# Where the residual of a feed-forward is fetched and added: a change in the order of loads around seven block products

## The chip, the core and the metric

The kernel runs on one core of a Trainium2 chip, as one launch. The metric is the device time of that core in microseconds, as the median of several runs. A core has TensorE for matrix products (PE; its weight loads are listed as PEld), VectorE (DVE), ScalarE (ACT), GpSimd (POOL) and SyncE (SP), which here issues nearly all DMAs. Every engine works through its own instructions in order and waits on semaphores.

## What is computed

One layer of a decoder trunk on 1024 prompt tokens and 64 sample tokens: a half-step feed-forward, a token mixer, a second half-step feed-forward and a last norm.

```python
def swiglu(x, w_in, w_out):
    gu = x @ w_in
    g, u = gu[..., :D_FF], gu[..., D_FF:]
    return (jax.nn.silu(g) * u) @ w_out
...
x = x + 0.5 * swiglu(rmsnorm(x, norm_ffn1[l]), ffn1_w_in[l], ffn1_w_out[l])
...
x = x + mix
x = x + 0.5 * swiglu(rmsnorm(x, norm_ffn2[l]), ffn2_w_in[l], ffn2_w_out[l])
```

D_MODEL is 1024 and D_FF is 2816. All inputs are float32. The change is in code that both feed-forwards use, so it acts twice.

## The kernel before

**Tokens and precision.** The 1088 tokens are two halves of 512 and 576, and each half is once more two equal parts of columns (256 or 288). Activations lie transposed: 128 channels on the partitions, tokens along the free axis. A float32 product is made from three float32r products: each operand is split into a high part (ScalarE's copy into float32r) and a low part (VectorE's subtraction of the high part from the source), and high x high, high x low and low x high are summed in PSUM.

**First product of a feed-forward (`ffn_in`, L546, and `wino`, L476).** Each hidden tile of 128 channels is made by Winograd's variant of Strassen's method: seven block products instead of eight, in the order 1, 2, 6, 5, 7, 3, 4 (L42). They share three PSUM banks, A for 1, 6, 7 and 4, B for 2, and C for 5 and 3. So a bank's sum must be copied out before a later product may add to it. The function `after0` (L550) does so for the first half: behind product 2 VectorE adds (L565), GpSimd adds the two column parts (L562), and ScalarE makes the SiLU (L567); behind product 6 ScalarE copies bank A into v (L569). Product 7, two products after 6, adds to A again. Most hidden tiles are made for both halves in one go, so that `xs` has two entries. The last tile (number 21) is made for one half after the other, each with a single entry in `xs`. This is the "one-half tile". `after0` has the first half alone, so its one-half tile comes once in each feed-forward.

**Second product (`second`, L740).** The product with `w_out` uses the same method, over pairs of hidden tiles, in the order 1, 2, 5, 6, 4, 7, 3 (L744). For each of the first six there are four units m = 0 to 3, written (p,m) below. Such a unit is 11 steps k of three matmuls for each of the two halves, 66 matmuls. Its weights come in three blocks kb = 0, 4 and 8; the generator `weights` (L791) loads raw tiles (`raw`, L770, issue L774), sums them on GpSimd where the method asks for it (L805, L809, L814; after product 4 also `fourth`, L821), and splits the sum (`parts`, high part on ACT L787, low part on DVE L788). The operands X of a product are 11 tiles each, hidden sums that the kernel had written to DRAM: `fetch_X` (L750) loads them (L760, named hr or hp) and `split_X` (L764) splits them on ACT (L767) and DVE (L768). For the next product, up to three tiles are fetched after each unit (L921 and L922), and the rest before that product begins (L905).

**Leaving a unit (`leave`, L858).** Each unit's two PSUM results are scaled by 0.5 and added on VectorE (L863) to four accumulators. These are a and b for the output tiles m and 4 + m, each with two token parts f and s.

**Residual parts.** The residual x lies in DRAM (`xspill`). One quarter of it, for b in part s, is loaded straight into the accumulator after product 6 (L882). The other three quarters go through a tile xo: `old` (L823) loads it with two DMAs (L827), and a GpSimd add (L833) follows later. `old` is called after a unit of product 6 (a, part f), and twice after a unit of product 7 (b part f, a part s). The list `late_` keeps the adds until the next unit has gone through its last weight block, kb = 8 (L852).

**What sets the order of instructions.** The kernel is written as one Python program. The framework's planner then gives each engine its order: at each point it takes, of the instructions whose inputs and buffers are ready by its own reckoning, the one traced first. So instructions with free inputs and buffers, weight loads above all, move ahead of what stands before them in the text. `pin` (`keep_in_program_order`) holds one instruction behind the instruction that was traced last on the same engine. The GpSimd adds and sums of the second product are all pinned, and so are the xo loads and ACT's high parts of X; L882 is not. Buffers come in rings by tag: `act` has 42 buffers (for hr and hh of most steps, xo, the weight sums that several products need, and more), `pair` has 8 (hp), `wraw` 6 (raw weights), `wsum` 4. `tick` (L159) only starts side work, such as norms and output transposes, when the kernel's own count of TensorE time has reached it.

**The end of the second product.** After product 7, `run` (L899) adds what is left in `late_`, calls `half` for each half (it starts the next norm, or in the second feed-forward the output transposes, named ptf), and does product 3 for one half after the other.

Of the kernel before, what the change touches and what calls it, by code (L numbers as in the profile page):

```python
# [11 lines left out]
AF = mybir.ActivationFunctionType  # L12
# [53 lines left out]
def tile_hybrid_pool_ssd_macaron(  # L66
# [11 lines left out]
    dma = nc.sync.dma_start  # L78
# [467 lines left out]
    def ffn_in(wi, ff, xs):  # L546

        out = {}

        def after0(p, i, bk):  # L550

            A, B, C = bk
            n = NPAIR[0]
            f, s_ = slice(0, n), slice(n, 2 * n)
            if p == "1":
                out[i] = o = {"g": fx(name="g"), "t": fx(name="t"), "v": fx(name="v")}
                S.copy(o["t"][:, : 2 * n], A)
                return
            g, t, v = out[i]["g"], out[i]["t"], out[i]["v"]

            def halves(o, x):
                G.tensor_tensor(o, x[:, f], x[:, s_], op=ALU.add)  # L562

            if p == "2":
                V.tensor_tensor(g[:, : 2 * n], B, t[:, : 2 * n], op=ALU.add)  # L565
                halves(g[:, f], g)
                S.activation(g[:, f], g[:, f], AF.Silu)  # L567
            elif p == "6":
                S.copy(v[:, : 2 * n], A)  # L569
            elif p == "5":  # L570
                S.copy(t[:, : 2 * n], C)
            elif p == "7":
                V.tensor_tensor(t[:, : 2 * n], A, t[:, : 2 * n], op=ALU.add)
                halves(t[:, f], t)
            elif p == "3":
                V.tensor_tensor(v[:, : 2 * n], C, v[:, : 2 * n], op=ALU.add)
                halves(g[:, s_], v)
                S.activation(g[:, s_], g[:, s_], AF.Silu)
            else:
                S.copy(t[:, s_], A[:, s_])  # L580
                V.tensor_tensor(t[:, s_], A[:, f], t[:, s_], op=ALU.add)
                V.tensor_tensor(g[:, f], g[:, f], t[:, s_], op=ALU.mult)
                G.tensor_tensor(g[:, s_], g[:, s_], t[:, f], op=ALU.mult)
                hidden(0, ff, g)

        def after(p, i, bk):
            h = xs[i][0]
            if h == 0:
                return after0(p, i, bk)
            n = NPAIR[h]  # L590
            A, B, C = (b[:, :n] if b is not None else None for b in bk)
            if p == "1":
                t = fx(name="t")
                out[i] = o = {"g": fx(name="g"), "t1": t[:, :n], "t5": t[:, :n], "t2": t[:, n : 2 * n]}
                S.copy(o["t1"], A)
                return
            o = out[i]
            g1, g2 = o["g"][:, :n], o["g"][:, n : 2 * n]
            if p == "2":
                V.tensor_tensor(g1, B, o["t1"], op=ALU.add)  # L600
                S.activation(g1, g1, AF.Silu)
            elif p == "6":
                S.copy(o["t2"], A)
            elif p == "5":
                S.copy(o["t5"], C)
            elif p == "7":
                V.tensor_tensor(o["t5"], A, o["t5"], op=ALU.add)
            elif p == "3":
                V.tensor_tensor(g2, C, o["t2"], op=ALU.add)
                S.activation(g2, g2, AF.Silu)  # L610
            else:
                V.tensor_tensor(g1, g1, A, op=ALU.mult)
                G.tensor_tensor(g2, g2, o["t5"], op=ALU.mult)
                hidden(h, ff, o["g"])

        wino(wino_weights(wi, 0, 4, 4, ff * P, FF + ff * P), 4, xs, after)
# [123 lines left out]
    def second(wo, after, half):  # L740
# [4 lines left out]
        X = {p: [] for p in order}  # L745
        T1 = [None] * 4
        xt = [[None] * KD for _ in HALVES]
        raws, held, late_ = [], {}, []

        def fetch_X(p, n):  # L750
            for k in range(len(X[p]), min(len(X[p]) + n, NK2)):
# [69 lines left out]
                pin(G.tensor_tensor(a, x, a, op=ALU.subtract))  # L821

        def old(m, q, col):  # L823
            t = act((P, 576), name="xo")
            for h in HALVES:
                n, at = NPAIR[h], HALF_AT[h]
                pin(dma(t[:, at : at + n], xspill[h][4 * q + m][:, col * n : (col + 1) * n]))  # L827

            def put():
                for h in HALVES:  # L830
                    n, at = NPAIR[h], HALF_AT[h]
                    o = xt[h][4 * q + m][:, col * n : (col + 1) * n]
                    pin(G.tensor_tensor(o, o, t[:, at : at + n], op=ALU.add))  # L833

            late_.append(put)

        def unit(p, m, hs, ws):
            pts = [psum("pd", "po" + p)[:, : NPAIR[h]] for h in hs]
            for kb, nk, wh, wl in ws:
                if kb and len(hs) == 2 and (p, m) == ("1", 0):  # L840
                    split_X(kb + 4)
                elif kb == 8:
                    split_X()
                for kk in range(nk):
                    k = kb + kk
                    for j, (W_, lo_) in enumerate(((wh, 0), (wh, 1), (wl, 0))):
                        for h, pt in zip(hs, pts):
                            at = HALF_AT[h]
                            mm(pt, W_[:, kk, :], X[p][k][lo_][:, at : at + NPAIR[h]],
                               start=k == 0 and j == 0, stop=k == NK2 - 1 and j == 2)  # L850
                    tick()
                if kb == 8:  # L852
                    while late_:
                        late_.pop(0)()
            for h, pt in zip(hs, pts):
                leave(p, m, h, pt)

        def leave(p, m, h, pt):  # L858
            n, at = NPAIR[h], HALF_AT[h]
            f, s_ = slice(0, n), slice(n, 2 * n)  # L860

            def add(out, prior):
                V.scalar_tensor_tensor(out, pt, 0.5, prior, op0=ALU.mult, op1=ALU.add)  # L863

            if p == "1":
                if T1[m] is None:
                    T1[m] = act((P, 576), name="t1")
                S.activation(T1[m][:, at : at + n], pt, AF.Copy, scale=0.5)
                return
            if p == "2":  # L870
                xt[h][m] = fx(name="x")
            elif p == "5":
                xt[h][4 + m] = fx(name="x")
            t, a, b = T1[m][:, at : at + n], xt[h][m], xt[h][4 + m]
            if p == "2":
                add(a[:, f], t)
            elif p == "5":
                add(b[:, s_], t)
            elif p == "6":
                add(a[:, s_], b[:, s_])  # L880
                add(b[:, f], t)
                dma(b[:, s_], xspill[h][4 + m][:, s_])  # L882
            elif p == "4":
                add(b[:, f], b[:, f])
                pin(G.tensor_tensor(b[:, s_], b[:, s_], a[:, s_], op=ALU.add))
            elif p == "7":
                add(b[:, f], b[:, f])
                add(b[:, s_], b[:, s_])
            else:
                add(a[:, s_], a[:, s_])  # L890
# [8 lines left out]
        def run(side):  # L899
            fetch_X("1", NK2)  # L900
            split_X(4)
            for p, nxt in zip(order[:-1], order[1:]):
                if p != "1":
                    split_X(8)
                fetch_X(p, NK2)  # L905
                for m in range(4):
                    unit(p, m, HALVES, weights(p, m))
                    if p == "6":
                        old(m, 0, 0)
                    elif p == "7":  # L910
                        old(m, 1, 0)
                        old(m, 0, 1)
                    if p == "4":
                        fourth(m)
                    if side and p == "2" and m == 0:
                        finish(side)
                    while p == "1" and hlast:
                        hlast.pop(0)()
                    while p == "1" and m == 2 and hsums:
                        finish(hsums.pop(0))  # L920
                    n = AHEAD[nxt] - len(X[nxt])  # L921
                    fetch_X(nxt, min(n, 3))  # L922
            split_X(8)
            fetch_X("3", NK2)
            while late_:
                late_.pop(0)()
            for h in HALVES:
                half(h, xt[h])
            kept = {m: [] for m in range(4)}

            def keep(m):
                for w in weights("3", m):
                    kept[m].append(w)
                    yield w

            for h in HALVES:
                for m in range(4):
                    unit("3", m, [h], kept[m] if h else keep(m))
                after(h, xt[h])
# [1080 lines left out]
```

## Time and profile before

| | |
|---|---|
| median of 3 runs | 2925.12 us (2923.38 to 2926.3) |
| the profiled execution's own time | 2925.94 us |
| its span, first to last instruction | 2924.2 us |
| mean granted TensorE clock in it | 0.985 |
| second product of the first feed-forward | from 527 us, with its last unit's results leaving at 800 us |
| second product of the second feed-forward | from 2639 us, with its last unit's results leaving at 2909 us |

A row of a timeline reads: start, duration, engine, line of the kernel, operation, output<-inputs, shape, how many were merged, and in brackets how long the engine had been idle and what ended that. An engine name with q, such as SPq, means an instruction of its queue: SP's DMA issues are there, and their duration is that of the issue, not of the transfer. A row of windows gives for one stretch of the span each engine's busy time and number of instructions, then the granted TensorE clock (1.00 is full speed), the mean busy share of the 16 DMA engines and what they moved. A row for one line of the kernel gives the shortest, median and longest duration in ns.

### The profile page before, as it was taken

How to read it: one execution, taken by the hardware profiler on the slowest of the kernel's cores; microseconds unless marked ns; L12 is line 12 of the kernel's file. 1: busy time of each engine (PE TensorE's matmuls, PEld its weight loads, DVE VectorE, ACT ScalarE, POOL GpSimd, SP SyncE). 2: the span in 40 equal slices, each digit the busy share in tenths (PEclk: the TensorE clock that was granted, in tenths of full speed). 3: DMA queues.
4: the chain of work that ended last, by engine and by line, in shares of the span. 5: the costliest groups of instructions: out<-in, count | busy, mean ns of one | idle time of the engine just before them, and what ended most of it. 6: DMA issues, size and time to landing. Idle time of an engine off the chain costs nothing. (4 is left out here: it accounts for less than half of the span.)

```text
span 2924.2 us, 54556 instructions
## 1 busy us (share of the span) xinstructions
PE 2798.1 (96%) x19834; PEld 2614.3 (89%) x19834; DVE 1857.1 (64%) x2848; ACT 1400.7 (48%) x3086; POOL 1370.1 (47%) x1424
## 2 busy tenths in 40 slices
PE   7999999998999999999999999898999999999987
PEld 6999999998889999999998887677999999999987
DVE  6656556666884586866766767766665444456675
ACT  5444444433444555554555566566233344444333
POOL 6456566146542364554622333332235676561562
PEclk9999999999999999999999999999999999999999
DMA  4466445677545455543366577785774333246783
GB/s 132 147 196 210 158 147 177 209 216 234 167 115 170 150 179 169 184 140 125 101 234 214 186 230 240 248 263 185 241 238 136 114 118 102 88 132 192 214 241 105
DMA packets 567437, 515.25 MB, mean 176 GB/s; under 512 B 37876, under 2 KB 436072, under 8 KB 567160
## 3 DMA queue, kind: packets, MB, share of 16 engines
q1 hardware_dynamic: 564848, 507.31, 55.3%
q10 hardware_dynamic: 2320, 4.46, 0.4%
q8 instruction: 156, 2.56, 0.4%
q14 instruction: 113, 0.93, 0.1%
HBM read 363.51 MB, written 148.36 MB: 175 GB/s over the span
## 5 line engine op out<-in xcount | busy, mean ns | idle before, releaser
L167 PE MATMUL pw<-X,wh 128*128 128x288 f32 (+2 forms) x2832 | 626.2, 310 | 4.0 <-ACT v L569 4.0
L167 PEld LDWEIGHTS pw<-X,wh 128*128 128x128 f32 x2832 | 462.0, 189 | 26.2 <-ACT v L569 4.8
L167 PE MATMUL pw<-X,wl 128*128 128x288 f32 (+1 forms) x1644 | 473.3, 288 | 0.0
L167 PE MATMUL pw<-hl,wh 128*128 128x256 f32 (+1 forms) x1536 | 395.2, 330 | 0.6 <-ACT wh L452 0.4
L453 DVE TENSOR_TENSOR wl<-s,wh 128x512 fp32r<-128x512 f32 x288 | 232.0, 807 | 253.7 <-ACT wh L452 241.7
L446 POOL TENSOR_TENSOR s<-wraw,wraw 128x512 f32<-128x512 f32 x144 | 199.5, 1386 | 337.7 <-DVE wl L453 224.0
L167 PE MATMUL pw<-hi,wh 128*128 128x288 f32 x1120 | 331.2, 296 | 0.0
L167 PE MATMUL pw<-hi,wl 128*128 128x288 f32 x1120 | 330.4, 295 | 0.0
L167 PE MATMUL pw<-lo,wh 128*128 128x288 f32 x1120 | 330.2, 295 | 0.0
L167 PEld LDWEIGHTS pw<-X,wl 128*128 128x128 f32 x1644 | 311.7, 190 | 0.0
L167 PE MATMUL pw<-hl,wl 128*128 128x256 f32 x1072 | 301.8, 282 | 1.2 <-DVE wl L453 1.2
L167 PEld LDWEIGHTS pw<-hl,wh 128*128 128x128 f32 x1536 | 260.4, 190 | 22.0 <-ACT wh L452 0.6
L452 ACT ACTIVATE wh<-s 128x512 fp32r<-128x512 f32 x288 | 181.1, 630 | 163.9 <-PE pw L167 139.9
L453 DVE TENSOR_TENSOR wl<-wraw,wh 128x512 fp32r<-128x512 f32 x216 | 170.5, 789 | 135.8 <-ACT wh L452 127.2
L452 ACT ACTIVATE wh<-wraw 128x512 fp32r<-128x512 f32 x216 | 135.6, 628 | 174.6 <-PE pw L167 151.4
L167 PEld LDWEIGHTS pw<-hi,wh 128*128 128x128 f32 x1120 | 211.2, 189 | 6.4
L167 PEld LDWEIGHTS pw<-lo,wh 128*128 128x128 f32 x1120 | 211.2, 189 | 0.0
L167 PEld LDWEIGHTS pw<-hi,wl 128*128 128x128 f32 x1120 | 210.7, 188 | 0.0
L167 PEld LDWEIGHTS pw<-hl,wl 128*128 128x128 f32 x1072 | 204.7, 191 | 1.4 <-DVE wl L453 1.4
L167 PE MATMUL po<-hr,wh 128*128 128x256 f32 (+1 forms) x848 | 188.2, 293 | 10.3 <-DVE hr L768 10.2
L167 PE MATMUL po<-hh,wh 128*128 128x256 f32 (+1 forms) x848 | 186.8, 291 | 6.7 <-ACT hh L767 6.3
L167 PE MATMUL po<-hh,wl 128*128 128x256 f32 (+1 forms) x848 | 186.0, 290 | 0.5 <-DVE wl L788 0.3
(400 smaller groups left out, 6850.8 us busy)
## 6 DMA issues: line engine op xcount, KB each, us to landing
wraw<-in_ffn_w_in_dram SPq DMA_DIRECT2D x188, 256.0 KB
wraw<-in_w_in_dram SPq DMA_DIRECT2D x144, 256.0 KB
wh<-part SPq DMA_DIRECT2D x116, 256.0 KB
wl<-part SPq DMA_DIRECT2D x116, 256.0 KB
hr<-hb SPq DMA_DIRECT2D x106, 272.0 KB
wraw<-in_ffn_w_out_dram SPq DMA_DIRECT2D x96, 256.0 KB
hb<-g SPq DMA_DIRECT2D x66, 288.0 KB
hb<-g SPq DMA_DIRECT2D x66, 256.0 KB
```

What stands on the lines that cost most here:

```text
L167: T.matmul(out, lhsT, rhs, start=start, stop=stop, skip_group_check=free)
L446: G.tensor_tensor(t, a, b, op=op)
L452: S.activation(wh, a, AF.Copy)
L453: V.tensor_tensor(wl, a, wh.bitcast(F32), op=ALU.subtract)
```

## The change

Three edits, all in code that both feed-forwards run.

1. In `after0`, when the tile is made for one half alone, the SiLU of part f is no longer issued behind product 2, but behind product 6, pinned after the copy of bank A.
2. `old` no longer loads. It puts a function (`reload_`, the former body) on a list `olds`. The load of the quarter that goes straight into b (L882) goes on that list as well, and is now pinned. The list is worked off in the next unit, behind the matmuls of its block kb = 4; working it off also puts the adds on `late_`.
3. `late_` is worked off behind the last weight block of a unit, after the loop. After product 7, both lists are emptied before `half`.

```diff
             if p == "2":
                 V.tensor_tensor(g[:, : 2 * n], B, t[:, : 2 * n], op=ALU.add)
                 halves(g[:, f], g)
-                S.activation(g[:, f], g[:, f], AF.Silu)
+                if len(xs) > 1:
+                    S.activation(g[:, f], g[:, f], AF.Silu)
             elif p == "6":
                 S.copy(v[:, : 2 * n], A)
+                if len(xs) == 1:
+                    tc.keep_in_program_order(S.activation(g[:, f], g[:, f], AF.Silu))
...
         def old(m, q, col):
+            olds.append(lambda: reload_(m, q, col))
+
+        def reload_(m, q, col):
             t = act((P, 576), name="xo")
             for h in HALVES:
                 n, at = NPAIR[h], HALF_AT[h]
...
                     tick()
-                if kb == 8:
-                    while late_:
-                        late_.pop(0)()
+                if kb == 4:
+                    while olds:
+                        olds.pop(0)()
+            while late_:
+                late_.pop(0)()
             for h, pt in zip(hs, pts):
                 leave(p, m, h, pt)
...
             elif p == "6":
                 add(a[:, s_], b[:, s_])
                 add(b[:, f], t)
-                dma(b[:, s_], xspill[h][4 + m][:, s_])
+                olds.append(lambda: pin(dma(b[:, s_], xspill[h][4 + m][:, s_])))
...
             fetch_X("3", NK2)
-            while late_:
-                late_.pop(0)()
+            for q in (olds, late_):
+                while q:
+                    q.pop(0)()
             for h in HALVES:
                 half(h, xt[h])
```

More of the change, by code (lines that the diff above doesn't have):

```diff
@@ L747, in second @@
         xt = [[None] * KD for _ in HALVES]
-        raws, held, late_ = [], {}, []
+        raws, held, late_, olds = [], {}, [], []
         def fetch_X(p, n):
```

## The prediction

> **What bounds the kernel now.** I read the page first, then TensorE's waits, then windows over the two places that the diff touches, then the timelines of SP, GpSimd (POOL), VectorE (DVE) and ScalarE (ACT) there.
>
> ```profile
> PE 2798.1 (96%) x19834; PEld 2614.3 (89%) x19834; DVE 1857.1 (64%) x2848; ACT 1400.7 (48%) x3086; POOL 1370.1 (47%) x1424
> PE po L167 <- ACT wh L787: 15.5, 7, 3.8
> PE po L167 <- DVE hr L768: 10.2, 20, 1.9
> PE po L167 <- ACT hh L767: 6.3, 5, 2.9
> PE pw L167 <- ACT v L569: 4.0, 3, 2.0
> ```
>
> TensorE is busy 96% of the span, so a change can only take away its waits and the stretches in which it runs slowly. The wait rows read: who waited, for whom, total us, times, longest. The matmuls of the second product carry the name po; their three largest waits sum to 32.0 us. The wait for the copy v (L569) is the half tile's.
>
> ```profile
> 576.00:592.00 16.00, 16.00 (x131) 16.00 (x130) 9.15 (x17) 6.87 (x12) 0.00 (x0) 1.00 0.55 160
> 644.20:757.10 112.90, 98.92 (x729) 96.45 (x728) 77.95 (x99) 38.43 (x67) 69.75 (x58) 0.94 0.75 219
> 2752.60:2865.30 112.70, 100.13 (x728) 97.05 (x727) 78.55 (x99) 37.79 (x66) 69.59 (x58) 0.94 0.74 220
> 677.70:691.80 14.10, 8.82 (x62) 7.95 (x61) 8.80 (x11) 2.97 (x6) 9.18 (x9) 0.96 0.69 209
> 691.80:716.60 24.80, 24.80 (x192) 24.75 (x191) 22.50 (x23) 9.89 (x17) 22.28 (x16) 0.96 0.75 214
> 716.60:737.40 20.80, 17.07 (x133) 16.42 (x131) 12.81 (x17) 6.45 (x12) 11.67 (x11) 1.00 1.04 300
> ```
>
> Columns: window, length, busy time (count) of PE, PEld, DVE, ACT, POOL, then granted clock, DMA share, GB/s. In products 2 and 5 TensorE takes 16.00/131 = 0.122 us per matmul, so a unit of 66 matmuls lasts 8.06 us. Products 6, 4 and 7, from the end of unit (6,0) to the end of (7,3), have 729 matmuls, worth 89.0 us, and take 112.9: 23.9 us too many in the first feed-forward, and 112.7 - 728 x 0.122 = 23.9 in the second. These 48 us are nearly all that the edit of the second product can win. I write (p,m) for unit m of product p.
>
> **The change part by part.** *The half tile's SiLU.*
>
> ```profile
> 508.06 0.42 ACT L567 ACTIVATE g<-g 128x256 f32<-128x256 f32 x1 [2.82 <-POOL g L562]
> 508.38 0.61 ACT L452 ACTIVATE wh<-s 128x512 fp32r<-128x512 f32 x1
> 508.90 0.56 ACT L569 COPY v<-pw 128x512 f32<-128x512 f32 x1
> 509.08 0.72 DVE L453 TENSOR_TENSOR wl<-s,wh 128x512 fp32r<-128x512 f32 x1 [1.64 <-ACT wh L452]
> 509.51 0.67 PE L167 MATMUL pw<-X,wh 128*128 128x512 f32 x1 [2.00 <-ACT v L569]
> 509.50:514.00 4.50, 4.49 (x17) 3.85 (x18) 3.33 (x4) 1.60 (x3) 2.09 (x2) 0.62 0.57 179
> 2621.00:2626.00 5.00, 5.00 (x19) 4.34 (x20) 3.92 (x6) 2.21 (x4) 2.40 (x2) 0.66 0.63 201
> ```
>
> ACT stands 2.82 us at the SiLU, which waits for POOL's sum; behind it are a weight part (L452) and the copy of v, which empties the bank that product 7 wants. TensorE stands 2.00 us, then runs at clock 0.62 for 4.5 us, which loses 0.38 x 4.5 = 1.7. In the second feed-forward the wait is about 1.8 (the rest of L569's 4.0 holds one other small wait) and the loss 0.34 x 5 = 1.7. With the copy first, 3.7 and 3.5 are at stake. Not all comes back: the L452 before the copy makes product 7's own weight, whose low part VectorE finishes at 509.80. If L452 still stands behind the SiLU, TensorE starts at 508.38 + 0.61 = 508.99 and saves 0.5; if it goes ahead, it can start about when the copy is done. The planner had put L452 ahead of the copy, so ahead of the SiLU is the nearer case. I take 2.5 per feed-forward, bounds 0.5 and 3.7: **5.0**. The SiLU itself then comes later; its reader is product 4's multiply, two products on, so that costs nothing; without that cover it would cost its 0.42.
>
> The Trainium skill ("TensorE: Matmul & The Clock Gate", What's actually happening) has the clock halve only after an idle window of about 3.4 us. The clock of 0.62 behind a wait of 2.00 says that shorter waits suffice here. By the page the edit would be worth 3.8 at most instead of 7.2, and my 5.0, cut in that proportion, 2.6; the sum would be 2.4 less.
>
> *The loads of the residual parts.* Nothing is added or removed: per feed-forward 8 loads into b (L882), 24 into xo (L827) and 24 POOL adds (L833). The adds keep their place on POOL, since the point behind block kb=8 is the unit's end in both versions and adds and weight sums are all pinned. Only the loads move on SP, from behind unit m to behind the kb=4 weights of unit m+1. So the operand fetches (L760) traced between, three at most per unit, now come ahead of them.
>
> ```profile
> 670.80 0.90 SPq L827 DMA_DIRECT2D xo<-xspill  x2
> 678.47 1.03 SPq L882 DMA_DIRECT2D x<-xspill  x2
> 679.55 0.90 SPq L827 DMA_DIRECT2D xo<-xspill  x2
> 680.50 1.38 SPq L760 DMA_DIRECT2D hr<-hb  x3
> 684.41 0.66 ACT L767 ACTIVATE hh<-hr 128x544 fp32r<-128x544 f32 x1 [5.10 <-DMA hr<-hb]
> 685.12 0.52 PE L167 MATMUL po<-hh,wh 128*128 128x256 f32 x2 [2.86 <-ACT hh L767]
> 679.42 1.15 DVE L788 TENSOR_TENSOR wl<-wraw,wh 128x384 fp32r<-128x384 f32 x2
> 685.10 1.05 DVE L768 TENSOR_TENSOR hr<-hr,hh 128x544 fp32r<-128x544 f32 x1 [4.53 <-ACT hh L767]
> 687.79 3.24 DVE L768 TENSOR_TENSOR hr<-hr,hh 128x544 fp32r<-128x544 f32 x2
> ```
>
> This is the place that matters. At 678.47 SP issues L882, which waited for unit (6,3) to leave its bank; the three hr behind it are k = 8 to 10 of product 4. They land at 684.4, when (4,0) has stood 2.86 us, and VectorE then splits them slowly beside POOL, so (4,0) waits again. The window from 677.7 shows it: 14.10 us with 8.82 busy. The hr and xo share one ring of buffers, and on SP they appear strictly in traced order (xo, hr, xo, hr), while fetches from other rings run ahead. In the new order these three hr follow the xo of unit (6,2), issued at 670.80. So I expect them at about 671.7, nine us earlier, landed before 678, split from 680.6 on (end of L788) at 0.71 each (the minimum of L768, quoted below), ready at 682.7. Then (4,0) takes 8.06 us and ends at 685.8 instead of 691.8.
>
> How much of these 6 us survives is set by POOL, whose chain does not move:
>
> ```profile
> 682.03 0.72 POOL L833 TENSOR_TENSOR x<-x,xo 128x256 f32<-128x256 f32 x1 [5.65 <-DMA xo<-xspill]
> 711.12 1.62 POOL L814 TENSOR_TENSOR ws<-ws,wraw 128x512 f32<-128x512 f32 x1
> L768 DVE TENSOR_TENSOR hr<-hr,hh x21: 710/1055/1808, 665.9 to 763.2; 128x544 fp32r<-128x544 f32 x21
> L821 POOL TENSOR_TENSOR ws<-ws,ws x24: 1279/1664/1794, 685.5 to 2817.7; 128x512 f32<-128x512 f32 x16, 128x384 f32<-128x384 f32 x8
> ```
>
> From 682.03 POOL works without a pause through the last adds of product 6 and all of product 4's sums until 711.12, when it makes the first weight of product 7. TensorE started (7,0) near 716.6: the window up to there holds 192 of the 198 matmuls of (4,1) to (4,3), a few records being missing. Now it would be there at 716.6 - 6.0 - 1.4 = 709.2 (the 1.4 is the slow stretch in that window: 24.8 us for matmuls worth 23.4). The weight is ready no sooner than 711.12 + 1.62 + 0.61 (ACT's part, as L452 above) + about 0.72 (VectorE's part undisturbed, as L453 above) = 714.1; with three VectorE splits out of POOL's way, the difference of 1.79 and 1.28 (maximum and minimum of L821) three times, 712.6. The gain at (7,0) is 716.6 - 712.6 = 4.0; bounds 0 (VectorE and POOL full) and 7.4 (TensorE alone). Twice: **8.0**. What is late next is POOL's first weight of product 7.
>
> *Product 6 otherwise.*
>
> ```profile
> 657.12 0.83 SPq L827 DMA_DIRECT2D xo<-xspill  x2
> 661.52 1.47 POOL L833 TENSOR_TENSOR x<-x,xo 128x256 f32<-128x256 f32 x2 [7.55 <-DMA xo<-xspill]
> 662.95 3.90 POOL L809 TENSOR_TENSOR ws<-ws,wraw 128x512 f32<-128x512 f32 x3
> ```
>
> The longest wait of all (3.8, for wh) comes about so: POOL stands at the add of (6,1), because its xo was issued at 657.12 and landed at 661.5, and the sums for (6,3) stand behind it. The xo still comes after L882 and the add still before the sums. I give this 0, with bounds of -4.4 and +2. The loss: behind the waiting L882 now stand on SP the kb=8 weights of unit m+1 too, unless the planner issues them ahead, as it does with other weights; TensorE would wait one landing for them (657.12 to 661.5, 4.4 us). The gain: a landing half as long.
>
> *Product 7 and the end.*
>
> ```profile
> 723.46 6.31 SPq L827 DMA_DIRECT2D xo<-xspill  x8
> 731.11 1.48 SPq L774 DMA_DIRECT2D ws<-in_ffn_w_out_dram  x3
> 730.29 4.23 POOL L833 TENSOR_TENSOR x<-x,xo 128x256 f32<-128x256 f32 x4 [1.80 <-DMA xo<-xspill]
> 735.46 3.90 POOL L814 TENSOR_TENSOR ws<-ws,wraw 128x512 f32<-128x512 f32 x3 [0.94 <-DMA ws<-in_ffn_w_out_dram]
> 741.63 3.77 POOL L833 TENSOR_TENSOR x<-x,xo 128x256 f32<-128x256 f32 x4 [2.27 <-DVE x L863]
> 757.88 4.18 POOL L833 TENSOR_TENSOR x<-x,xo 128x256 f32<-128x256 f32 x4 [2.89 <-DVE x L863]
> ```
>
> Eight xo, those of (7,0) and (7,1), stand ahead of the ws of (7,2) while the DMA share is 1.04. The second four now come behind the kb=4 ws of (7,2), so those land some 4 x 0.5 = 2 us earlier; POOL saves its 0.94, as its add until 734.5 stays ahead. Against it, the first four may push back the last ws of (7,1). I take 1.0, bounds -2 and +4: twice, **2.0**. After (7,3) the last four xo follow three hr; they were waiting for VectorE at 757.88 anyway, so I charge 0.5 (issue of three hr 1.4, less some slack), bounds 0 and 2: **-1.0**.
>
> Sum: 5.0 + 8.0 + 2.0 - 1.0 = **14 us**. The profiled execution took 2925.9 (span 2924.2), so 2911.9; the median of the runs is 2925.1, which makes **2911**.
>
> **The rivals.** *A: VectorE and POOL hold product 4.* In 691.8:716.6 both are busy 22 of 24.8 us, and VectorE's splits take 1.81 at most against 0.71 alone. If the 6 us won at (4,0) go into VectorE waiting for POOL, (7,0) starts where it did and about 5 us of the SiLU remain: 2920. For it speaks that POOL has no gap; against it that TensorE never stood in that window. The Trainium skill ("SBUF — State Buffer", Who interferes with whom) makes this a rule: a tensor_tensor with both inputs in SBUF and a POOL operation that reads SBUF exclude each other. Both durations grow here, as it says.
>
> *B: everything comes loose.* (4,0) wins its 7.4, product 7 its 4, the SiLU 3.7, each twice, less 1: 29 us, 2896. The POOL row at 711.12 speaks against it.
>
> *C: slower, by late residuals.* All POOL work is in strict order, so a late xo holds the next weights. Landing took 6.7 us in product 7 (723.46 to 730.2). With xo (7,1) behind the ws at 731.6, it is issued near 732 and needed at 741.6: this decides from a landing of 9 us. If ring or queue make each of the three adds 3 us late, and the last one too (the output transposes in the second feed-forward read it), it is 12 us per feed-forward, 24 in all, less the 13 won before: 2936. The slack of 9 us speaks against it.
>
> *D: the fetches do not move.* If the three hr wait for something other than the order of the ring, the loads are hidden as before and only the SiLU acts: 2920, as A.
>
> **How the numbers follow.** Forecast 0.53 (its own range 2903 to 2919), A and D together 0.18, B 0.12, C 0.17. One can tell from no change what differs by 0.2%, 5.8 us. The forecast, B and a little of A (0.02) are faster: 0.67. The rest of A and D and a mild C (0.02) are within: 0.18. C is slower: 0.15. The range, 2898 to 2930, leaves out most of C and the far end of B.
>
> **What would show it.** Right: the three hr of product 4 stand on SP before the last L882 of product 6; the wait for hh L767 in (4,0) is gone; POOL has a pause, or TensorE a wait for wh, at (7,0); v L569 is gone from TensorE's waits. Wrong: hr issued behind the last xo as now; POOL waiting for xo in product 7 beyond the leave of its unit; a transpose ptf waiting for the last adds.

## The result, and the profile after

| | before | changed |
|---|---|---|
| median of 8 runs each, same chip | 2924.25 us | 2933.78 us (2929.12 to 2937.95) |
| ratio | | 1.0032, 95% interval 1.002 to 1.0045 |
| profiled execution, its span | 2925.9, 2924.2 us | 2937.9, 2936.1 us |
| mean granted clock in it | 0.985 | 0.979 |

The change makes the kernel slower by 9.5 us (6 to 13 by the interval), outside the predicted range of 2898 to 2930. The page of the changed kernel, its busy line, then its waits of TensorE (waited for: total us, times, longest). In the changed kernel's numbering ScalarE's high part of X is L770, VectorE's low part of X L771, the weight's high part L790, its low part L791, the copy v L570, product 7's weight sum on POOL L817, `fourth`'s L824, the add of xo L839, product 4's second add L893:

```profile
PE 2801.3 (95%) x19834; PEld 2619.4 (89%) x19834; DVE 1845.3 (63%) x2848; ACT 1400.6 (48%) x3086; POOL 1369.5 (47%) x1424
```

```profile
PE po L167 <- ACT wh L790: 37.1, 8, 9.3
...
PE po L167 <- DVE hr L771: 6.4, 15, 1.3
...
PE po L167 <- ACT hh L770: 1.2, 3, 0.4
...
PE pw L167 <- ACT v L570: 1.0, 1, 1.0
```

Three of the four waits of before that the prediction set out from shrank as intended: X's low parts from 10.2 to 6.4, its high parts from 6.3 to 1.2, the copy v from 4.0 to 1.0. The fourth, for the weight's high part, grew from 15.5 to 37.1, and its longest from 3.8 to 9.3.

Where in the span? TensorE has the same instructions in nearly the same order in all kernels of this study, so I take the start of the same instruction, by its number, in each profile. A stretch runs from the start of its first instruction to that of its last. The table gives the length of a stretch in the profile of before, and by how much it is longer (+) in a second profile of before (run b2, below) and in the changed kernel.

| stretch, first / second feed-forward | TensorE's instruction numbers | before, us | before again | changed |
|---|---|---|---|---|
| start-up and mixing up to the half tile | 0 to 3180 | 503.2 | +4.3 | +4.4 |
| half tile's SiLU | 3180 to 3240 / 17700 to 17880 | 13.5 / 30.9 | -0.1 / 0.0 | -2.3 / -2.5 |
| product 6 | 4000 to 4310 / 18640 to 18950 | 45.2 / 46.0 | +0.6 / -0.5 | -0.7 / -0.2 |
| product 4 | 4310 to 4560 / 18950 to 19200 | 39.0 / 38.1 | -0.4 / +0.3 | -7.2 / -6.8 |
| start of (7,0) | 4560 to 4640 / 19200 to 19280 | 10.6 / 10.4 | +0.3 / +0.3 | +11.7 / +10.5 |
| rest of product 7 | 4640 to 4840 / 19280 to 19480 | 32.3 / 32.6 | -0.7 / -0.6 | +1.0 / +2.0 |
| between the feed-forwards | 5240 to 17700 | 1784.8 | -2.0 | +3.1 |

Two profiles of one kernel differ by 4.3 us in the start-up, and by 2.8 us between instructions 3240 and 4000. So what the changed kernel shows there tells nothing. In the stretches that the diff touches the two agree within 0.7. But run e1 below, whose second product is that of before, differs from before by up to 2.0 in a stretch of product 4 or 7, so a difference of 2 us there is not to be read. Two are far larger: product 4 wins 7 us in each feed-forward, and the start of (7,0) loses 11.

The timelines of the changed kernel, first at (4,0):

```profile
671.22 1.38 SPq L763 DMA_DIRECT2D hr<-hb  x3
...
675.49 1.01 SPq L890 DMA_DIRECT2D x<-xspill  x2
676.55 2.28 SPq L833 DMA_DIRECT2D xo<-xspill  x2
...
678.52 0.66 ACT L770 ACTIVATE hh<-hr 128x544 fp32r<-128x544 f32 x1 [1.70 <-DMA hr<-hb]
...
680.46 0.72 DVE L771 TENSOR_TENSOR hr<-hr,hh 128x544 fp32r<-128x544 f32 x1
```

The three hr of product 4 are issued at 671.22, ahead of the upper halves (L890) and xo that stood ahead of them before, and the last is split at 681.2. And at (7,0), TensorE, ScalarE, POOL and SP:

```profile
708.36 0.41 PE L167 MATMUL po<-hh,wl 128*128 128x256 f32 x2
718.07 1.28 PE L167 MATMUL po<-hp,wh 128*128 128x256 f32 x4 [9.30 <-ACT wh L790]
...
742.43 1.28 PE L167 MATMUL po<-hp,wh 128*128 128x256 f32 x4 [4.80 <-ACT wh L790]
...
715.28 1.38 ACT L770 ACTIVATE hh<-hr 128x544 fp32r<-128x544 f32 x2 [12.66 <-DMA hr<-hb]
716.84 0.66 ACT L770 ACTIVATE hh<-hr 128x544 fp32r<-128x544 f32 x1 [0.17 <-DMA hr<-hb]
717.40 1.13 ACT L790 ACTIVATE wh<-ws 128x512 fp32r<-128x512 f32 x2
...
706.30 3.51 POOL L824 TENSOR_TENSOR ws<-ws,ws 128x512 f32<-128x512 f32 x3
709.77 1.26 POOL L817 TENSOR_TENSOR ws<-ws,wraw 128x512 f32<-128x512 f32 x1
...
708.89 1.32 SPq L777 DMA_DIRECT2D ws<-in_ffn_w_out_dram  x2
710.26 1.45 SPq L763 DMA_DIRECT2D hr<-hb  x3
```

POOL has the first sum for (7,0) done at 709.77 + 1.26 = 711.03. ScalarE makes its high part only at 717.40. Between them ScalarE stands 12.66 us at a high part of X: three hr of product 7 (k = 6 to 8) that SP issued at 710.26. On SP these stand behind loads into sum buffers (L777). A buffer comes free when POOL has made a sum, and the second load of the row at 708.89 goes out with the end of the last L824, at 706.30 + 3.51 = 709.81. In the kernel before, the same three hr stood further ahead among those loads:

```profile
708.51 1.41 SPq L760 DMA_DIRECT2D hr<-hb  x3
...
712.77 2.17 ACT L767 ACTIVATE hh<-hr 128x544 fp32r<-128x544 f32 x3 [4.17 <-DMA hr<-hb]
714.85 0.61 ACT L787 ACTIVATE wh<-ws 128x512 fp32r<-128x512 f32 x1
...
716.48 0.66 PE L167 MATMUL po<-hp,wh 128*128 128x256 f32 x4
```

So the high part of the weight of (7,0) is begun 2.55 us later than before (717.40 against 714.85), though TensorE comes 7 to 8 us sooner. In the kernel before TensorE went into (7,0) at 716.48 without waiting for it. Windows of the changed kernel behind that wait, and over POOL's part of product 4:

```profile
718.07:724.00 5.93, 5.55 (x26) 5.23 (x27) 4.45 (x6) 0.99 (x2) 2.74 (x2) 0.57 0.69 181
...
682.77:711.03 28.26, 25.62 (x203) 25.18 (x202) 19.48 (x19) 7.38 (x13) 28.26 (x23) 1.00 0.53 148
```

Behind the long wait TensorE's clock is 0.57 for 5.93 us, which costs 0.43 x 5.93 = 2.5 us. TensorE begins the stretch at 701.22 against 709.09 in the kernel before, 7.9 sooner; it begins (7,0) at 718.07 against 716.48, 1.6 later; with the 2.5 that makes 12.0, against 11.7 lost in that stretch. And POOL is busy for 28.26 of 28.26 us.

### The profile page after: what moved, and what is told of

Same layout as the page of the kernel before. It is cut to its first block, busy times and chain, and to the rows that moved or that the text cites. A ratio compares the mean times of both kernels' runs of the same rounds, so it can differ in the third digit from the quotient of the medians.

```text
span 2936.1 us, 54574 instructions
## 1 busy us (share of the span) xinstructions
PE 2801.3 (95%) x19834; PEld 2619.4 (89%) x19834; DVE 1845.3 (63%) x2848; ACT 1400.6 (48%) x3086; POOL 1369.5 (47%) x1424
## 5 line engine op out<-in xcount | busy, mean ns | idle before, releaser
L167 PEld LDWEIGHTS pw<-hl,wh 128*128 128x128 f32 x1536 | 259.3, 190 | 22.8 <-ACT t L574 1.7
L167 PE MATMUL pso<-yhl,wh 128*128 128x288 f32 (+1 forms) x768 | 180.7, 337 | 5.5 <-ACT acc L1829 3.5
```

What stands on the lines that cost most here:

```text
L167: T.matmul(out, lhsT, rhs, start=start, stop=stop, skip_group_check=free)
```

## The experiments

Theory T: the SiLU edit gains; the moved loads of product 6 gain in product 4 and lose more at (7,0), because the weight's high part stands on ScalarE behind the three late high parts of X. Rivals: the loss comes from product 7's residuals that now come late (A, the prediction's C), or the difference has nothing to do with the parts (N).

### The parts, each alone

Run e1 is the kernel before with edit 1 of the change. Run e2 is the changed kernel without it:

```diff
-                if len(xs) > 1:
-                    S.activation(g[:, f], g[:, f], AF.Silu)
+                S.activation(g[:, f], g[:, f], AF.Silu)
...
-                if len(xs) == 1:
-                    tc.keep_in_program_order(S.activation(g[:, f], g[:, f], AF.Silu))
```

> The kernel before with the SiLU edit alone; all loads and adds of the second product where they were. Theory T (the edit of the SiLU gains what the drift between the two traces shows, about 3.7 and 3.6 us in the two networks, and the loads lose more than that): 2924 - 7 = 2917 us, ratio 0.9975, and (7,0) starts as before, with a wait of under 1 us for its weight. Rival N (the difference between the two kernels does not come from the change's parts, but from the start-up and mix stages): no part alone goes beyond 0.2%, 2918 to 2930.

> The changed kernel with the SiLU put back to where it was; the loads and adds of the second product as changed. Theory T: slower than the changed kernel by the SiLU's 7 us, 2934 + 7 = 2941, ratio 1.0055 (1.002 to 1.007), with a wait of TensorE of 7 to 10 us for the high part of the weight at (7,0) in both networks. Rival N: 2918 to 2930.

Run e3 is the changed kernel with product 7's loads as early as before; run e4 the same for product 6's:

```diff
                         old(m, 1, 0)
                         old(m, 0, 1)
+                        while olds:
+                            olds.pop(0)()
```

```diff
-                olds.append(lambda: pin(dma(b[:, s_], xspill[h][4 + m][:, s_])))
+                dma(b[:, s_], xspill[h][4 + m][:, s_])
...
                         old(m, 0, 0)
+                        while olds:
+                            olds.pop(0)()
```

> The changed kernel, but product 7's two old residual parts are loaded as soon as they were before; product 6's old parts and its upper halves stay moved, and so does the add at a unit's end. Theory T (the loss sits at (7,0): SP's order there, with the three loads of product 7's k = 6 to 8 behind the loads that wait for the weight sums of POOL, comes from product 6's moved parts): the long wait at (7,0) stays at 7 to 10 us, and the time is that of the changed kernel within 4 us, 2930 to 2938. Rival A (the loss comes from product 7's residuals that now come late): product 4's gain stays and the loss goes, 2900 to 2912.

> The changed kernel, but product 6's loads (old parts and upper halves) are issued where they were before; product 7's stay moved, and so does the add at a unit's end. Theory T: product 4 and (7,0) go as in the kernel before (a wait for its high part of X of about 3 us in (4,0), under 1 us at (7,0)), and the time is that of the SiLU edit alone within 5 us, 2912 to 2922. Rival A: the loss is here, 2928 to 2940, with waits of TensorE inside product 7 or after it, behind POOL's adds of the old parts.

| run | median, us | ratio to before (95%) |
|---|---|---|
| before | 2925.53 | |
| e1, SiLU alone | 2922.1 | 0.9995 (0.9985 to 1.0005) |
| e2, loads alone | 2934.76 | 1.0031 (1.002 to 1.0042) |
| e3, SiLU and product 6's loads | 2935.66 | 1.0039 (1.0024 to 1.0054) |
| e4, SiLU and product 7's loads | 2922.24 | 0.9989 (0.9977 to 1.0) |

The loss goes with product 6's loads: it is there in e3 and gone in e4, so A falls, and so does N. TensorE's timelines at (7,0), first of e3, then of e4:

```profile
718.65 1.28 PE L167 MATMUL po<-hp,wh 128*128 128x256 f32 x4 [7.41 <-ACT wh L790]
```

```profile
680.22 0.52 PE L167 MATMUL po<-hh,wh 128*128 128x256 f32 x2 [1.98 <-ACT hh L770]
...
711.69 0.78 PE L167 MATMUL po<-hp,wh 128*128 128x256 f32 x4 [1.40 <-ACT wh L790]
```

In e4 the wait for X in (4,0) is back, and the one at (7,0) is 1.40. The SiLU missed its 7 us both ways: e1 can't be told from before, and e2, which lacks the edit, is level with the changed kernel (2934.76 against 2933.78) where 2941 was expected, with a wait of 8.73 at (7,0).

By the stretches of the table, the twelve profiles of this study with the edit have -2.0 to -2.3 in the first feed-forward and -2.5 or -2.6 in the second, and the five without it (two of before, e2, and e7 and f5 below) 0 to -1.2 and 0 to -1.5. The difference of the means is 1.8 and 2.0, 3.7 us together. The spread of the five has a reason. All of them wait 1.5 to 2.2 us for v in each feed-forward, but the slow clock follows in six of these ten places only. In e7 TensorE waits 2.10 us in the first feed-forward, and the clock behind it stays at 1.00, where the kernel before had 0.62:

```profile
510.43 0.50 PE L167 MATMUL pw<-X,wh 128*128 128x512 f32 x1 [2.10 <-ACT v L569]
...
510.43:514.93 4.50, 4.50 (x25) 3.83 (x26) 4.27 (x6) 2.21 (x4) 2.72 (x3) 1.00 0.56 175
```

In the four places without the slow clock the stretch is 1.1 to 1.5 us shorter than before. None of the twelve profiles with the edit has this wait or a slow clock in the stretch. Most have a shorter wait further on instead, in the changed kernel one for the copy t (L574), which stands on ScalarE behind the SiLU:

```profile
512.45 0.42 ACT L572 ACTIVATE g<-g 128x256 f32<-128x256 f32 x1 [0.89 <-POOL g L562]
...
513.91 0.50 PE L167 MATMUL pw<-hl,wh 128*128 128x512 f32 x1 [0.58 <-ACT t L574]
```

### What stands ahead of the weight at (7,0)

Run e5 changes one thing in the changed kernel: ScalarE's high parts for k = 6 to 8 of product 7 come behind the first two weight blocks of (7,0).

```diff
-                elif kb == 8:
+                elif kb == 4 and (p, m) == ("7", 0):
+                    split_X(9)
+                elif kb == 8 and (p, m) != ("4", 3):
                     split_X()
...
                 if p != "1":
-                    split_X(8)
+                    split_X(6 if p == "7" else 8)
```

> The changed kernel with one thing in another order on ScalarE: the high parts of X of product 7 for k = 6 to 8 (hh) stand behind the high parts of the first two weight chunks of (7,0), not ahead of them; SP's loads keep their order. Theory T (at (7,0) the high part of the weight stands in ScalarE's queue behind these three hh, whose loads land only at 715.25 us; POOL's sum for it is there at 711.03): the wait of TensorE at (7,0) falls from 9.30 and 8.66 us to 3 to 5.5 us, the time from 2934 to 2914 to 2924, so about even with before or a little faster. Rival P (POOL's chain and the loads that wait for its sums hold all of product 7): the wait only moves to the next chunks of (7,0) and to (7,1), 2930 to 2936.

Run e6 fetches product 7's X in another order, in the changed kernel; e7 does so in the kernel before:

```diff
-AHEAD = {'2': 11, '5': 11, '6': 8, '4': 8, '7': 10, '3': 8}
+AHEAD = {'2': 11, '5': 11, '6': 8, '4': 8, '7': 8, '3': 8}
...
-                    fetch_X(nxt, min(n, 3))
+                    fetch_X(nxt, min(n, 5 if nxt == "7" and m == 1 else 3))
```

> The changed kernel with product 7's parts of X for k = 3 to 7 fetched behind (4,1) and k = 8 to 10 at product 7's start, instead of k = 3 to 5 behind (4,1), 6 to 8 behind (4,2), 9 behind (4,3) and 10 at the start. On SP the loads for k = 6 and 7 then stand far ahead of the loads that wait for the weight sums, and those for 8 to 10 have their hh behind the weights of (7,0) on ScalarE. Theory T: as with the hh moved alone, a wait of 3 to 5.5 us at (7,0), and the loads of (7,0)'s third chunk go out about 1 us earlier: 2908 to 2922. Rival P: 2930 to 2936.

> The kernel before with the same fetch order of product 7's parts of X as in the run beside it, and nothing else. Theory T: the order at (7,0) costs the kernel before little, since TensorE comes there only at 716.3 us (a wait of 0.32 us): 2918 to 2925, ratio 0.998 to 1.000. Rival P: no difference either. If it gains over 6 us, the fetch order is worth something in another place than at (7,0), and the run with it on the changed kernel doesn't tell for T.

Run b2 is the kernel before, unaltered.

> The kernel before once more, for a second profile of it. Between 1750 and 2110 us the SiLU edit alone lost 5.6 us against the first profile of before, and the loads alone lost 4.7 us, with the same order of TensorE's instructions there. If this is a spread from run to run, the second profile differs from the first by 2 to 5 us in that stretch; if that stage takes back what a stage ahead of it gained, it repeats within 1 us.

Before was 2926.79 here; e5 2927.16 (ratio 1.0005, 0.9994 to 1.0016), e6 2926.94 (0.9994, 0.998 to 1.0008), e7 2922.72 (0.9985, 0.9974 to 0.9996); b2's one time was 2924.83. e5 and e6 lie between the ranges of T and of its rival P, so the time decides for neither; e7 is where T had it. Against the first profile of before, b2 moved by 1.0 us between 1750 and 2110 us and by 1.6 between 1740 and 2054, which lies between the two expectations; and it differs by 4.3 us in the start-up, so a few us in one stretch of one profile prove nothing.

TensorE and ScalarE in e5 at (7,0):

```profile
709.38 1.27 PE L167 MATMUL po<-hp,wh 128*128 128x256 f32 x4 [2.09 <-ACT wh L790]
...
736.57 1.16 PE L167 MATMUL po<-hp,wh 128*128 128x256 f32 x4 [4.58 <-ACT wh L790]
...
708.70 0.63 ACT L790 ACTIVATE wh<-ws 128x512 fp32r<-128x512 f32 x1 [8.71 <-POOL ws L817]
...
713.15 2.14 ACT L770 ACTIVATE hh<-hr 128x544 fp32r<-128x544 f32 x3 [1.97 <-DMA hr<-hb]
```

The wait falls from 9.30 to 2.09, and the weight's high part now waits for POOL's sum alone. T is right about ScalarE's queue: nearly all of the loss against before goes when the queue is reordered. But the kernel is only level with before, and the 7 us of product 4 are gone all the same. T doesn't say where. In e6, TensorE and POOL, then a window over POOL's part of product 4:

```profile
701.80 0.52 PE L167 MATMUL po<-hp,wl 128*128 128x256 f32 x2 [2.47 <-DVE wl L791]
...
737.84 1.28 PE L167 MATMUL po<-hp,wh 128*128 128x256 f32 x4 [4.84 <-ACT wh L790]
...
708.86 1.27 POOL L817 TENSOR_TENSOR ws<-ws,wraw 128x512 f32<-128x512 f32 x1
...
730.93 4.46 POOL L839 TENSOR_TENSOR x<-x,xo 128x256 f32<-128x256 f32 x4 [1.14 <-DVE wl L791]
735.35 4.09 POOL L817 TENSOR_TENSOR ws<-ws,wraw 128x512 f32<-128x512 f32 x3
```

```profile
680.47:710.12 29.65, 27.18 (x204) 26.79 (x203) 22.75 (x22) 8.48 (x15) 29.65 (x23) 0.94 0.56 160
```

At (7,0) there is now no wait worth a row; one of 2.47 us is in (4,3), for a low part that VectorE makes. POOL works for 29.65 of 29.65 us through product 4 and begins the first sum of (7,0) at 708.86, only 2.3 us before its 711.12 in the kernel before. The first sum for (7,2) comes at 735.35, behind four adds of xo, against 735.46 before: to a tenth where it was. So a second theory, Q: POOL's own chain, in a fixed order, holds product 7, and what TensorE wins ahead of it is given back there. The rival L: the loads of the weights, through their four sum buffers, hold it.

### POOL's adds on VectorE

Run f1 is e6 with product 4's second add on VectorE and out of the fixed order, f2 with the adds of xo there too. They compute the same.

```diff
-                pin(G.tensor_tensor(b[:, s_], b[:, s_], a[:, s_], op=ALU.add))
+                V.tensor_tensor(b[:, s_], b[:, s_], a[:, s_], op=ALU.add)
```

```diff
-                    pin(G.tensor_tensor(o, o, t[:, at : at + n], op=ALU.add))
+                    V.tensor_tensor(o, o, t[:, at : at + n], op=ALU.add)
```

> The run with product 7's parts of X fetched early, plus one edit: product 4's second add (x plus x of the upper half, two per unit, eight in all) goes to VectorE and is no longer in POOL's fixed order. In the profile without this edit POOL works back to back through product 4 (first sum 684.13, last 707.89 us), its eight such adds take about 9.3 us of that, and its first sum for (7,0) begins at 708.86 while TensorE is done with product 4 at some 699.5. Theory Q (what TensorE gains in product 4 is given back at (7,0) because POOL's own chain through product 4 did not get shorter): POOL's first sum for (7,0) begins 5 to 9 us earlier, the waits and slow stretches of (7,0) shrink by 4 to 6 us in each network, 2912 to 2920. Rival L (the weight loads, which go through four sum buffers and busy transfer engines, set product 7): no gain, 2922 to 2930.

> As the run beside it, and the adds of the old parts (four for each unit) go to VectorE too. Theory Q: the sum of POOL for (7,2) no longer stands behind four adds that take 4.4 us (730.93 to 735.35 us), the wait of 4.84 us at (7,2) falls to 1 to 3, a further 2 to 6 us for both networks: 2908 to 2917. Rival L: (7,2)'s sum waits for its loads instead, as the run beside it within 3 us.

Run f3 is the kernel before with the SiLU edit and the fetch order of e7, f4 is f3 with product 4's add on VectorE.

> The kernel before with the SiLU edit and product 7's parts of X fetched early; its loads and adds of old parts as before. The two edits alone gave ratios of 0.9995 and 0.9985. If they add up, 0.998, 2921 against 2926.5, and a version ahead of both kernels; if the early fetch only moved a wait, 0.999 to 1.000.

> As the run beside it (SiLU edit and early fetch on the kernel before), and product 4's second add on VectorE. Theory Q: without the moved loads TensorE comes to (7,0) late enough for POOL's sum, so a shorter chain of POOL brings less here than with them, 0 to 4 us: 2917 to 2922. Rival L: 0.

The last three put both adds on VectorE in the kernel before (f5), in the changed kernel (f6), and in f3 (f7).

> The kernel before with product 4's second add and the adds of the old parts on VectorE, and nothing else: what the adds alone are worth without the change. With the moved loads and the early fetch they brought 2927 - 2893 = 34 us. If the adds hold POOL's chain whatever the loads do, most of that comes here too: 2895 to 2905. If they matter only because the change lets TensorE arrive early (theory Q): 2908 to 2920.

> The changed kernel with the same adds on VectorE, its fetch order as it is. Theory T (the hh of product 7 ahead of the weight of (7,0) cost 7 to 11 us by themselves): a wait of 5 us or more at (7,0) stays, 2900 to 2912, 5 to 16 us behind the run with the early fetch (2893). Rival (POOL's chain was the only hindrance): no wait over 3 us at (7,0), 2889 to 2897.

> The kernel before with the SiLU edit, the early fetch and these adds on VectorE: everything of the fastest run (2893) but the moved loads of old parts. It tells what the moved loads are worth once neither POOL nor the hh hold (7,0): theory Q, the gain of product 4 is kept, so this run is 8 to 14 us slower than 2893, 2901 to 2907; rival (the gain of product 4 is given back whatever stands at (7,0)): 2889 to 2897.

| run | moved loads | fetch of X for 7 | adds on VectorE | median, us | ratio to before (95%) |
|---|---|---|---|---|---|
| f1 | yes | early | product 4's | 2909.91 | 0.9948 (0.9934 to 0.9962) |
| f2 | yes | early | all | 2893.32 | 0.9889 (0.9876 to 0.9903) |
| f3 | no | early | none | 2917.43 | 0.9974 (0.9964 to 0.9985) |
| f4 | no | early | product 4's | 2915.72 | 0.9962 (0.9947 to 0.9976) |
| f5 | no (nor the SiLU edit) | as before | all | 2908.6 | 0.9939 (0.9921 to 0.9957) |
| f6 | yes, the changed kernel | as before | all | 2892.22 | 0.9883 (0.9868 to 0.9898) |
| f7 | no | early | all | 2903.71 | 0.9924 (0.9906 to 0.9942) |

The kernel before ran 2924.73 beside f1 to f4 and 2925.08 beside f5 to f7. f1, f2, f4, f5 and f7 went as Q has it and not as L, three of them below the range expected (f1 by 2, f4 by 1, f2 by 15 us); f3 shows that SiLU and early fetch add up to a version 7 us ahead of before. f2 has no wait at (7,2) any more, as Q had it, but a new one in (7,1): an add of xo on VectorE now stands 10.74 us for its load, the weight's low part stands behind it, and TensorE waits 4.84 for that (f6 has it too, with 2.49 and, in the second feed-forward, 4.73). So the adds are not free on VectorE either. The pair that decides is f5 and f6: the whole change, put on top of the adds, gains 2908.6 - 2892.2 = 16.4 us, where without them it loses 9.5. And f2 is 10 us ahead of f7, which has all but the moved loads (by the ratios, since the two were run beside different runs of before). In f6, ScalarE and POOL at (7,0), then a window that ends there, in which TensorE never stops and POOL is busy 14.47 of 20.38 us:

```profile
695.50 1.38 ACT L770 ACTIVATE hh<-hr 128x544 fp32r<-128x544 f32 x2 [0.17 <-DMA hr<-hb]
696.79 1.14 ACT L790 ACTIVATE wh<-ws 128x512 fp32r<-128x512 f32 x2
...
686.98 1.77 POOL L817 TENSOR_TENSOR ws<-ws,wraw 128x512 f32<-128x512 f32 x1
```

```profile
676.62:697.00 20.38, 20.38 (x165) 20.38 (x164) 15.79 (x18) 7.34 (x14) 14.47 (x10) 1.00 0.87 241
```

Here T's expectation failed: with the fetch order of the changed kernel f6 has no wait over 3 us at (7,0) and is as fast as f2. The high parts of X still stand ahead of the weight on ScalarE, but they are done at 696.9: POOL's sum for (7,0) begins at 686.98 instead of 709.77, and the loads behind POOL's sums on SP go out earlier with it. So the two theories are one. POOL's lateness was what held (7,0); the queue on ScalarE was the way by which it reached the weight, and added to it. Either edit takes the loss away: e5 the queue, f6 the lateness.

How the adds weigh on the two engines, rows of one line of the kernel (min/median/max ns), first of the changed kernel, then of f6:

```profile
L893 POOL TENSOR_TENSOR x<-x,x x16: 742/1063/1292, 684.2 to 2820.4; 128x256 f32<-128x256 f32 x8, 128x288 f32<-128x288 f32 x8
```

```profile
L893 DVE TENSOR_TENSOR x<-x,x x16: 411/436/452, 650.7 to 2768.3; 128x256 f32<-128x256 f32 x8, 128x288 f32<-128x288 f32 x8
```

VectorE does such an add in 0.44 us where POOL takes 1.06. The eight of product 4 free 8 x 1.06 = 8.5 us of POOL's full 28, and in f1, which moves these alone, POOL's first sum for (7,0) begins at 700.12, 8.7 us sooner than in e6. In f6 it begins 22.8 us sooner than in the changed kernel, so there is more to it. POOL in the changed kernel, at the start of its full stretch, then in f6:

```profile
682.77 1.51 POOL L839 TENSOR_TENSOR x<-x,xo 128x256 f32<-128x256 f32 x2 [7.38 <-DMA xo<-xspill]
```

```profile
651.61 2.66 POOL L824 TENSOR_TENSOR ws<-ws,ws 128x512 f32<-128x512 f32 x2 [2.04 <-DVE x L893]
676.62 4.84 POOL L824 TENSOR_TENSOR ws<-ws,ws 128x512 f32<-128x512 f32 x3 [22.35 <-DVE hp L771]
```

In the changed kernel POOL stands 7.38 us at the last adds of product 6, and then makes the twelve sums of `fourth` (L824) before the first of product 7, though only product 3 needs them. In f6 no such add stands in POOL's order, six of the twelve sums are made by 654.3, and POOL has time to spare. How much of f6's gain is the shorter work and how much the freed order no run separates: none leaves the adds on POOL and frees their order.

The stretches of the runs that matter, in us against the first profile of before, first / second feed-forward:

| run | product 6 | product 4 | start of (7,0) | rest of product 7 |
|---|---|---|---|---|
| changed | -0.7 / -0.2 | -7.2 / -6.8 | +11.7 / +10.5 | +1.0 / +2.0 |
| e1 | -0.7 / -1.1 | -1.4 / +1.9 | +1.6 / -0.4 | +2.0 / -0.5 |
| e3 | +0.4 / 0.0 | -7.4 / -6.8 | +10.0 / +10.5 | +3.2 / +2.4 |
| e4 | +0.3 / -0.1 | -2.3 / +0.8 | +4.0 / -0.4 | -1.9 / -1.0 |
| e5 | +0.9 / +0.7 | -7.8 / -6.8 | +4.8 / +1.8 | +3.5 / +6.7 |
| e6 | +0.2 / -0.3 | -4.3 / -5.1 | +1.0 / +1.1 | +6.0 / +4.5 |
| f1 | -0.4 / +0.4 | -5.3 / -5.2 | +0.8 / -0.4 | -1.8 / -1.4 |
| f5 | -5.5 / -5.9 | +0.9 / 0.0 | -0.6 / -0.4 | +0.7 / -0.6 |
| f6 | -6.1 / -6.4 | -7.8 / -6.8 | -0.6 / -0.4 | -2.3 / -0.3 |
| f7 | -4.7 / -6.5 | +0.8 / +2.2 | -0.6 / -0.4 | -2.3 / -5.2 |

In e5 and e6 the gain of product 4 is returned in product 7, spread over its units. In f6 it is kept, and f7, without the moved loads, has none to keep. The adds of xo held product 6 as well: without them on POOL, its wait for the weight of (6,3) is gone, 6 us in each feed-forward.

## Why the prediction was wrong

**SiLU, 5.0 us.** Right in kind, 3.7 by the means of the stretches, which is too little for the runs of e1 and e2 to show. The wait is gone in both feed-forwards, but the sum took the slow clock behind it as certain, and it came in six of ten places; and "costs nothing" for the late SiLU was not quite so, since TensorE now waits 0.58 for the copy t behind it. The Trainium skill ("TensorE: Matmul & The Clock Gate", What's actually happening) has the clock halve only after an idle window of about 3.4 us, and the prediction's estimate by it was 2.6. The six places, with the clock at 0.52 to 0.66 behind waits of 1.8 to 2.1 us, speak against it here.

**Product 4.** The mechanism was right, and its size too (7.2 and 6.8 won, 7.4 reckoned). The three hr were put at 671.7 and came at 671.22; ready at 682.7, they were at 681.2; TensorE was to be at (7,0) at 709.2, and its last matmul of product 4 started at 708.36. The long wait for hh is gone.

**The start of (7,0), 4.0 us each, bounds 0 to 7.4.** This is the step that failed. It had the weight ready at 712.6, from POOL's sum, ScalarE's part and VectorE's part. POOL's sum came at 711.03, as reckoned, but ScalarE's part not behind it at 711.1 but at 717.40. The step counted only the three operations that make the weight, and no queue in which they stand: three high parts of X ahead of it on ScalarE, behind loads that SP issues behind loads for POOL's sums. The rows of the kernel before (708.51, 712.77, 714.85, above) showed this row of three; in that kernel TensorE came at 716.48 and the high part was ready by then, so nobody waited for it. The bound of 0 was wrong as well: an earlier arrival can't cost by itself, but the planner had also moved the hr back on SP, and the wait has a slow clock behind it. The clock of 0.62 that the prediction read behind a wait of 2.00 us is there behind 9.30 too (0.57), and I charged nothing for it. Product 4 and this start together were to win 8.0 in the two feed-forwards and lost 4.5 and 3.7, which is 16 us of the 23.5 between the 14 forecast and the 9.5 lost. The prediction also had POOL without a pause up to 711.12; the kernel before has it busy 28.50 of those 29.09 us, which changes nothing here.

**Product 6, 0.** It held: -0.7 and -0.2. That its wait hangs on POOL's xo adds was read correctly; f5 shows what the adds there are worth (6 us each), but the change moves only the load, and the add stays on POOL.

**Product 7, +2.0.** No gain is to be seen: 1.0 and 2.0 us lost, which e1 reaches too. With product 7's loads left early (e3) it lost 3.2 and 2.4, and e4 wins 1.9 and 1.0 with these loads late. So their move may be worth a little, but it isn't shown: by the runs e4 is level with e1 (2922.24 against 2922.1). That POOL's chain makes the rest of the loss in product 7 is argued from e6 and f1.

**The end, -1.0.** Nothing is to be seen: the stretch behind product 7 in the second feed-forward (19480 to 19800) has the same length within 0.1.

**The rivals.** C had the sign, but not the mechanism: e3 keeps the loss without late residuals in product 7, e4 has them and loses nothing. A had VectorE and POOL holding product 4; POOL holds product 7, and product 4 does win. D fell with the hr at 671.22. The signs named beforehand came (hr ahead of the last load of an upper half, no wait for hh, a wait for wh at (7,0)), but a wait for wh was counted there as a mark of success. Its length had to be named.

## What to carry to other kernels

When an engine is to arrive earlier at a stage, follow each of its inputs there through every in-order queue, and not only through the operations that make it: what stands ahead, which load that waits for, and who releases that load's buffer. An engine that is busy without a gap for a whole stage (POOL in the changed kernel, 28.26 of 28.26 us) can hold the next stage, though its share of the span is 47%. Look at what it makes there, and who needs that first. A change that loses may stand behind another limit: with POOL's adds on VectorE, where such an add takes 0.44 us for 1.06, the same change gains 16 us, and f6 is 33 us ahead of the kernel before.

## What the runs showed of the hardware

Two profiles of the same kernel differ by 4.3 us in the first 505 us and by 2.8 us in another stretch, with ends only 1.2 us apart, so a drift between single profiles that is not tied to a named wait is worth little. After waits of 1.5 to 2.2 us in the same place TensorE's clock fell in six of ten cases (0.52 to 0.66 over the 3.5 to 5.0 us behind) and stayed at 1.00 in four; what decides between them was not settled. What lost 5.6 us in e1 between 1750 and 2110 us, with TensorE's order unaltered, was not settled.
